# A divergence of row distributions: a casting load issued ahead of the identity matrix, six row groups on chip, and new column ranges

## Chip, cores and metric

One core of a Trainium2 chip. The metric is the device time of one execution in microseconds. The kernel before took 98.53 us (median of four executions, 97.99 to 99.74).

## What is computed

For two arrays p and q of 1024 rows and 4096 columns (fp32, each row adds up to one), the Jensen-Shannon divergence of each row:

```
m = 0.5 * (p + q)
kl_pm = np.sum(p * np.log(p / (m + 1e-8) + 1e-8), axis=-1)
kl_qm = np.sum(q * np.log(q / (m + 1e-8) + 1e-8), axis=-1)
return (0.5 * (kl_pm + kl_qm)).astype(np.float32)
```

## The kernel before

The 1024 rows are eight row groups of 128 rows, one row on each partition. Within a group the columns are cut into ranges, and four tables (L20 to L59) give the widths for each group: LOADS (what one DMA brings), LOGS (what one logarithm of p and q takes), PRODUCTS (the buffer that holds the two logarithms) and SUMS (what one sum p + q takes). The ranges of a table are numbered through all groups. For row groups 0 to 5 a range goes this way:

- **Loads.** The first HW = 2 ranges (512 and 256 columns) are loaded as fp32, p on SP's queue (L171) and q on ScalarE's (L172). All others are loaded by GpSimd with a cast to fp16 (L184 for p, L185 for q), in the order of LOADS. Each row group has a buffer of its own, so nothing but the number of loads in flight holds these back: a load waits until the eighth load before it has landed.
- **F**: TensorE adds p and q into PSUM with two matmuls against the identity (L261), in blocks of 512 columns, p and then q of each block. For the first two ranges VectorE adds instead (**a**, L236).
- **p, q**: ScalarE takes the logarithms of p and q (L277); in the first SPLIT = 5 ranges p and q are two instructions, later one over both. **c**: ScalarE takes the logarithm of the sum, from PSUM (L295).
- **u, x**: VectorE subtracts c from both logarithms (L307) and multiplies by p and q (L317). **X**: TensorE adds up the products into an accumulator of 256 columns (L356), with half the identity as weights. **f**: VectorE adds up the 256 columns (L378).

Row groups 6 and 7 (APART) avoid the subtraction. **m** multiplies the logarithms by p and q at once (L324), **s** multiplies the sum by its logarithm (L335), and **M** and **S** add both up on TensorE. The last four s and the last m are instead added up along the row by VectorE itself (L339, L328), each starting from the value of the one before. At the very end ScalarE adds up the 256 columns of row group 7 (**A**, L367), and **f7** (L372) adds VectorE's part; then SP writes the result (L466). **W** are matmuls without use (L249).

Three lists written out by hand, ACT_ORDER, PE_ORDER and DVE_ORDER (L73 to L88), fix the order on each engine; `q12 c14` means the logarithm of range 12 of LOGS and then that of range 14 of SUMS. The loop at L435 walks through the three lists and issues each entry as soon as all it depends on has been issued (`after`, L401); each engine then works strictly in its order. Logarithms share AB_BUFS = 5 buffers, logarithms of sums C_BUFS = 4. GpSimd makes the identity (L177) ahead of its first load. For row group 7 the tables are:

```
LOADS     [2048, 2048],
LOGS      [768, 1024, 896, 512, 512, 384],
PRODUCTS  [768, 1024, 896, 512, 512, 384],
SUMS      [1536, 1408, 1152],
```

Of the kernel before, what the change touches and what calls it, by code (L numbers as in the profile page):

```python
# [12 lines left out]
SW = (1536, 1536)  # L13
AW = 256
AB_BUFS = 5
C_BUFS = 4

LOADS = [  # L20
    [512, 256, 832, 960, 768, 768],
    [512, 896, 832, 768, 1088],
    [1280, 1408, 1408],
    [1152, 1408, 1536],
    [1280, 1536, 1280],
    [1408, 1408, 1280],
    [256, 1536, 1536, 768],
    [2048, 2048],
]
LOGS = [  # L30
    [512, 256, 832, 960, 768, 768],
    [512, 896, 832, 768, 1088],
    [1280, 1408, 1408],
    [1152, 1408, 1536],
    [1280, 1536, 1280],
    [1408, 1408, 1280],
    [256, 1536, 1536, 768],
    [768, 1024, 896, 512, 512, 384],
]
PRODUCTS = [  # L40
    [512, 256, 832, 1728, 768],
    [512, 896, 832, 1856],
    [1280, 1408, 1408],
    [1152, 1408, 1536],
    [1280, 1536, 1280],
    [1408, 1408, 1280],
    [1792, 1536, 768],
    [768, 1024, 896, 512, 512, 384],
]
SUMS = [  # L50
    [512, 256, 448, 384, 384, 384, 960, 768],
    [512, 896, 832, 768, 1088],
    [1280, 1408, 1408],
    [1152, 1408, 1536],
    [1280, 1536, 1280],
    [1408, 1408, 1280],
    [256, 1536, 1280, 1024],
    [1536, 1408, 1152],
]  # L59
HW = 2  # L60
SPLIT = 5

APART = 6
FUSED_M = 1
FUSED_S = 4

# [2 lines left out]


ACT_ORDER = """  # L73
p0 q0 c0 p1 q1 c1 p2 q2 c2 c3 p3 q3 c4 c5 p4 q4 c6 q5 c7 q6 c8 q7 c9 q8 c10 q9 c11 q10 c12
q11 c13 q12 c14 q13 c15 q14 c16 q15 c17 q16 c18 c19 q17 q18 c20 c21 q19 c22 q20 c23 q21
c24 c25 q22 c26 q23 q24 c27 q25 c28 q26 c29 q27 q28 c30 q29 c31 q30 q31 q32 A7
"""
PE_ORDER = """
W30 F2 F3 X0 X1 F4 F5 X2 X3 F6 X4 X5 F7 F8 X6 F9 X7 F10 X8 F11 X9 F12 X10 X11 F13 W8 X12
F14 F15 X13 F16 X14 F17 X15 F18 X16 F19 X17 F20 X18 F21 X19 F22 X20 F23 X21 F24 F25 X22  # L80
F26 S25 X23 F27 F28 S26 X24 M21 F29 S27 M22 M23 F30 F31 M24 M25 W10 M26 W4 M27 M28
"""
DVE_ORDER = """
a0 a1 u0 x0 u1 x1 u2 u3 x2 x3 u4 u5 x4 x5 u6 x6 u7 x7 u8 x8 f0 u9 x9 u10 x10 u11 x11 u12
x12 u13 f1 x13 u14 x14 u15 x15 u16 x16 f2 u17 x17 u18 x18 u19 x19 f3 u20 x20 u21 x21 u22
f4 x22 u23 s25 x23 u24 s26 x24 m21 s27 f5 m22 s28 m23 s29 m24 f6 m25 s30 m26 s31 m27 m28
m29 f7
"""  # L88


# [1 line left out]
def kernel(  # L92
# [18 lines left out]
    fp32 = mybir.dt.float32  # L111
    fp16 = mybir.dt.float16
# [18 lines left out]
    split = loads[HW][1]  # L131
# [6 lines left out]
        return r[0] >= APART  # L138

    small = ctx.enter_context(tc.tile_pool(name="small", bufs=1))  # L140
    lnp = ctx.enter_context(tc.tile_pool(name="lnp", bufs=AB_BUFS))
    mid = ctx.enter_context(tc.tile_pool(name="mid", bufs=C_BUFS))
    psp = [
# [11 lines left out]
    data = []  # L155
    for g in range(n_rg):
        t16 = small.tile([P, 2, n_cols - (split if g == 0 else 0)], fp16, tag=f"pq{g}")
        data.append(t16)

    def pq(g, c0, w):  # L160
        if g == 0:
            for i in range(HW):
                if loads[i] == (g, c0, w):
                    return early[i]
            c0 -= split
            assert c0 >= 0
        return data[g][:, :, c0 : c0 + w]

    for i in range(HW):
# [41 lines left out]
    for g in range(n_rg):  # L211
        own = [o for o in dve_order if o == ("f", g) or (fused(*o) and range_of(*o)[0] == g)]
        if g < n_rg - 1 or act_folds:
            own = [o for o in own if o[0] != "f"] + [("f", g)]
        chain[g] = own

    ab, c, s, product, acc = {}, {}, {}, {}, {}
# [102 lines left out]
    def op_m(k):  # L320
        g, c0, w = prods[k]
        u = pq(g, c0, w)
        if not fused("m", k):
            nc.vector.tensor_tensor(out=ab[k], in0=u, in1=ab[k], op=Alu.mult)  # L324
            product["M", k] = ab[k]
            return
        before, now = next_run(("m", k), g)
        nc.vector.tensor_tensor_reduce(  # L328
            out=ab[k], in0=u, in1=ab[k], scale=0.5, scalar=before,
            op0=Alu.mult, op1=Alu.add, accum_out=now,  # L330
        )

    def op_s(j):
        if not fused("s", j):
            nc.vector.tensor_tensor(out=c[j], in0=s[j], in1=c[j], op=Alu.mult)  # L335
            product["S", j] = c[j].unsqueeze(1)
            return
        before, now = next_run(("s", j), parts[j][0])
        nc.vector.tensor_tensor_reduce(  # L339
            out=c[j], in0=s[j], in1=c[j], scale=-0.5, scalar=before,  # L340
            op0=Alu.mult, op1=Alu.add, accum_out=now,
        )

    def add_up(kind, i):
# [9 lines left out]
        for n, (t, b) in enumerate(todo):  # L354
# [6 lines left out]
                stop=(kind, i) == adds[g][-1] and n == len(todo) - 1,  # L361
            )

    def op_A(g):
        folded = small.tile([P, 1], fp32, tag="folded")
        unused = small.tile([P, AW], fp16, tag="unused")
        nc.scalar.activation(out=unused, in_=acc[g][:, :AW], func=Act.Copy, accum_out=folded)  # L367
        state["folded"] = folded

    def op_f(g):  # L370
        if act_folds and g == n_rg - 1:
            nc.vector.tensor_tensor(  # L372
                out=res[:, g : g + 1], in0=state["folded"], in1=state["last"][g], op=Alu.add
            )
            return
# [25 lines left out]
    def after(kind, i):  # L401
        if kind == "F" and i - 2 >= HW:
            return [("s" if apart(parts[i - 2]) else "c", i - 2)]
        if kind == "q" and i < SPLIT:
            return [("p", i)]
        if kind in "pq" and product_of(i) >= AB_BUFS:
            return ab_free(product_of(i) - AB_BUFS)
        if kind == "c":
            return [("a" if i < HW else "F", i)] + ([c_free(i - C_BUFS)] if i >= C_BUFS else [])
        if kind == "x":  # L410
            return [("u", i)]
        if kind == "u":
            return [("c", i)] + [("q", k) for k in range(NL) if overlap(logs[k], parts[i])]
        if kind == "m":
            return [("q", k) for k in range(NL) if overlap(logs[k], prods[i])]
        if kind == "s":
            return [("c", i)]
        if kind in "XMS":
            g = range_of(kind, i)[0]
            return [(kind.lower(), i)] + ([("f", g - 2)] if g >= 2 else [])  # L420
        if kind == "W":
            return []
        if kind == "f":
            if act_folds and i == n_rg - 1:
                return chain[i][:-1] + [("A", i)]
            return chain[i][: chain[i].index(("f", i))] + adds[i]
        if kind == "A":
            return adds[i]
        return []

    accumulator(0)
    ops = dict(a=op_a, F=op_F, p=op_p, q=op_q, c=op_c, u=op_u, x=op_x, m=op_m, s=op_s, f=op_f, A=op_A)
    queues = [list(pe_order), list(act_order), list(dve_order)]
    emitted = set()
    while any(queues):  # L435
        moved = False
# [21 lines left out]
    want |= {(k.upper(), i) for k, i in want if k in "xms" and not fused(k, i)}  # L458
    want |= {("f", g) for g in range(n_rg)} | {("p", i) for i in range(SPLIT)}
    if act_folds:  # L460
        want.add(("A", n_rg - 1))
    assert emitted == want
# [34 lines left out]
```

## Time and profile before

| | |
|---|---|
| median of four executions | 98.53 us (97.99 to 99.74) |
| the profiled execution | 99.74 us, of which its span is 97.0 |
| ScalarE (ACT) busy | 90.0 us, 93% |
| VectorE (DVE) busy | 81.8 us, 84% |
| TensorE (PE) busy | 71.4 us, 74% |
| cast loads (q0) | 16.39 MB, 89.3% of the 16 DMA engines' span |
| fp32 loads (q1 and q10) | 0.79 MB, 2.7% |
| read from HBM | 33.55 MB, 346 GB/s over the span |

The profile is of one execution, with times in microseconds from the start of the span. An engine is busy while an instruction of it runs; a row of the timeline has start, length, engine, line, operation, what is written and read, and in brackets the idle time before it and what ended it. POOL is GpSimd, SP the engine that issues p's first loads and the result. A DMA's time to landing runs from its issue to its completion.

### The profile page before, as it was taken

What the parts mean: (1) busy time and instruction counts of PE and PEld (TensorE: products, weight loads), DVE (VectorE), ACT (ScalarE), POOL (GpSimd) and SP (SyncE); (2) the same over time, 40 slices, a digit from 0 to 9 for tenths busy, and PEclk for the clock granted to TensorE, in tenths of its full rate; (3) what the DMA queues carried; (4) which work ended last, traced back from release to release, by engine and by line L of the source; (5) the groups of instructions that cost most, each with busy time, mean ns of one, the idle gap of its engine ahead of it and who ended that gap; (6) DMA issues with size and microseconds to landing.
All of it is one profiled execution on the core that took longest, in us unless ns stands there. A gap on an engine that the chain in (4) does not pass through costs nothing.

```text
span 97.0 us, 1327 instructions
## 1 busy us (share of the span) xinstructions
PE 71.4 (74%) x476; PEld 46.1 (48%) x476; DVE 81.8 (84%) x87; ACT 90.0 (93%) x74; POOL 29.3 (30%) x60
## 2 busy tenths in 40 slices
PE   4996686796686948786795884884966979797750
PEld 3774343454345425553461651652643766566520
DVE  2286887999958879898979989979999999999990
ACT  3696999999999999999999999999999999999960
POOL 6943466455232234224242322325400000000000
PEclk9999999999999999999999999999999999999997
DMA  2999999999999999999999999999999999200000
GB/s 47 317 163 204 206 204 209 206 211 210 214 209 215 209 210 215 211 211 211 214 210 212 211 214 208 209 208 212 210 209 217 211 216 216 51 0 3 0 0 2
DMA packets 8502, 17.25 MB, mean 178 GB/s; under 512 B 1072, under 2 KB 3888, under 8 KB 8496
## 3 DMA queue, kind: packets, MB, share of 16 engines
q0 software_dynamic: 7776, 16.39, 89.3%
q1 hardware_dynamic: 432, 0.40, 1.5%
q10 hardware_dynamic: 288, 0.39, 1.2%
q8 instruction: 3, 0.05, 0.2%
q14 instruction: 3, 0.02, 0.1%
HBM read 33.55 MB, written 0.00 MB: 346 GB/s over the span
## 4 chain that ended last, share of the span: by engine, by line
ACT 39%; issue 22%; DVE 13%; PE 2%; ACTq 0%; DVEq 0%
ACT ab_t L277 23%; ACT c_t L295 16%; DVE ab_t L307 5%; DVE t L317 4%; DVE c_t L335 2%; DVE c_t L339 1%; PE acc_t L356 1%; PE st L261 1%; DVE ab_t L324 1%; ACT unused L367 0%; DVE res L378 0%; ACTq L295 0%; DVE res L372 0%; ACTq L492 0%; DVEq L317 0%
## 5 line engine op out<-in xcount | busy, mean ns | idle before, releaser
L277 ACT ACTIVATE ab_t<-t 128x2816 f16<-128x2816 f16 (+15 forms) x38 | 62.5, 1684 | 2.1 <-DMA t<-in_q_dram 1.0
L261 PE MATMUL st<-t,ident 128*128 128x512 f16 (+4 forms) x144 | 33.4, 350 | 9.4 <-DMA t<-in_q_dram 8.4
L307 DVE TENSOR_TENSOR ab_t<-ab_t,c_t 128x2816 f16<-128x2816 f16 (+12 forms) x25 | 29.3, 1180 | 7.7 <-ACT c_t L295 6.9
L356 PEld LDWEIGHTS <-half 128*128 128x128 f16 x268 | 25.3, 97 | 20.5 <-issue 16.7
L295 ACT ACTIVATE c_t<-st 128x1408 f16<-128x1408 f32 (+13 forms) x30 | 32.2, 1096 | 0.0
L356 PE MATMUL acc_t<-t,half 128*128 128x256 f16 (+2 forms) x200 | 23.9, 264 | 8.9 <-DVE t L317 8.6
L317 DVE TENSOR_TENSOR t<-t,ab_t 128x2816 f16<-128x2816 f16 (+11 forms) x23 | 28.2, 1234 | 1.2
L261 PEld LDWEIGHTS <-ident 128*128 128x128 f16 x144 | 13.4, 97 | 23.1 <-issue 12.8
L185 POOL DMA_DIRECT2D t<-in_q_dram x27 | 14.4, 534 | 20.7 <-DMA t<-in_q_dram 20.6
L184 POOL DMA_DIRECT2D t<-in_p_dram x27 | 14.5, 538 | 19.6 <-DMA t<-in_p_dram 19.4
L356 PE MATMUL acc_t<-ab_t,half 128*128 128x256 f16 x68 | 8.8, 270 | 2.9 <-DVE ab_t L324 2.9
L324 DVE TENSOR_TENSOR ab_t<-t,ab_t 128x1536 f16<-128x1536 f16 (+5 forms) x8 | 9.3, 1172 | 0.1
L249 PE MATMUL acc_t<-ones,ident 128*128 128x256 f16 x30 | 6.2, 403 | 1.4 <-POOL ident masks.py:199 1.4
L249 PEld LDWEIGHTS <-ident 128*128 128x128 f16 x30 | 4.3, 145 | 3.0 <-POOL ident masks.py:199 1.4
L335 DVE TENSOR_TENSOR c_t<-st,c_t 128x256 f16<-128x256 f32 (+2 forms) x3 | 3.6, 1217 | 0.0
L236 DVE TENSOR_TENSOR s<-t 128x512 f32<-128x512 f32 (+1 forms) x2 | 1.1, 558 | 2.7 <-DMA t<-in_q_dram 2.7
L339 DVE CUSTOM_DVE_ANT_0 c_t<-st,c_t,run 128x1408 f16<-128x1408 f32 (+1 forms) x2 | 3.1, 1549 | 0.0
L339 DVE CUSTOM_DVE_ANT_0 c_t<-st,c_t 128x1024 f16<-128x1024 f32 (+1 forms) x2 | 3.0, 1484 | 0.0
L249 PE MATMUL acc_t<-ones,zero 128*128 128x256 f16 x22 | 2.9, 272 | 0.0
L175 ACT ACT_TABLE_LOAD x1 | 1.3, 1283 | 1.7 <-PEq L481 1.7
L378 DVE TENSOR_REDUCE res<-acc_t 128x1 f32<-128x256 f32 x6 | 2.5, 416 | 0.0
L249 PEld LDWEIGHTS <-zero 128*128 128x128 f16 x22 | 2.1, 98 | 0.2
(24 smaller groups left out, 10.5 us busy)
## 6 DMA issues: line engine op xcount, KB each, us to landing
t<-in_p_dram POOLq DMA_DIRECT2D x5, 352.0 KB, 12.6
t<-in_q_dram POOLq DMA_DIRECT2D x5, 352.0 KB, 12.8
t<-in_p_dram POOLq DMA_DIRECT2D x4, 384.0 KB, 11.8
t<-in_q_dram POOLq DMA_DIRECT2D x4, 384.0 KB, 12.0
t<-in_p_dram POOLq DMA_DIRECT2D x4, 320.0 KB, 13.0
t<-in_q_dram POOLq DMA_DIRECT2D x4, 320.0 KB, 12.8
t<-in_p_dram POOLq DMA_DIRECT2D x2, 512.0 KB, 13.2
t<-in_q_dram POOLq DMA_DIRECT2D x2, 512.0 KB, 14.4
```

The costliest lines, as they stand in the source:

```text
L184: nc.gpsimd.dma_start(out=v[:, 0, :], in_=pv[g, :, c0 : c0 + w])
L185: nc.gpsimd.dma_start(out=v[:, 1, :], in_=qv[g, :, c0 : c0 + w])
L249: nc.tensor.matmul(out=acc[g][:, :AW], lhsT=weights, rhs=ones, start=alone, stop=alone)
L261: nc.tensor.matmul(out=st[:, b : b + m], lhsT=ident, rhs=v[:, t, b : b + m], start=t == 0, stop=t == 1,)
L277: nc.scalar.activation(out=ab[k][:, which, o : o + w], in_=pq(g, c0, w)[:, which, :], func=Act.Ln, bias=TINY, scale=SHIFT,)
L295: nc.scalar.activation(out=c_t[:, :w], in_=s[j], func=Act.Ln, bias=SHIFT * 1e-8, scale=SHIFT * 0.5)
L307: nc.vector.tensor_tensor(out=v, in0=v, in1=c[j].unsqueeze(1).to_broadcast([P, 2, parts[j][2]]), op=Alu.subtract,)
L317: nc.vector.tensor_tensor(out=into, in0=u, in1=v, op=Alu.mult)
L324: nc.vector.tensor_tensor(out=ab[k], in0=u, in1=ab[k], op=Alu.mult)
L335: nc.vector.tensor_tensor(out=c[j], in0=s[j], in1=c[j], op=Alu.mult)
L339: nc.vector.tensor_tensor_reduce(out=c[j], in0=s[j], in1=c[j], scale=-0.5, scalar=before, op0=Alu.mult, op1=Alu.add, accum_out=now,)
L356: nc.tensor.matmul(out=acc[g][:, :m], lhsT=less if kind == "S" else half, rhs=v[:, t, b : b + m], start=(kind, i) == adds[g][0] and n == 0 ...
```

## The change

Three things at the start. GpSimd issues the first casting pair (now 864 columns) ahead of the memset and select that make the identity. The fp32 loads are 576 and 384 columns wide. The useless matmuls at the start are 22 for 30.

Row groups no longer have a buffer each: six buffers (DATA_BUFS) take turns, so the loads of groups 6 and 7 wait until the last sums of groups 0 and 1 are done. Load entries **L** stand in a list of their own in the issue loop. C_BUFS is 5 for 4. All four tables are new, and the three orders follow them; products are up to 2816 columns wide, so that one buffer takes two logarithms. The logarithms split in p and q are seven ranges for five, and five s for four are added up by VectorE itself.

At the end ScalarE's A takes VectorE's part as its bias (divided by 256, since it is added in each column) and writes the result itself; f7 goes. VectorE's f6 is its last instruction.

```diff
-C_BUFS = 4
+C_BUFS = 5
+DATA_BUFS = 6
 LOADS = [
-    [512, 256, 832, 960, 768, 768],
-    [512, 896, 832, 768, 1088],
-    [1280, 1408, 1408],
+    [576, 384, 864, 1088, 1184],
+    [1280, 1536, 1280],
     [1152, 1408, 1536],
-    [1280, 1536, 1280],
-    [1408, 1408, 1280],
-    [256, 1536, 1536, 768],
+    [1024, 1024, 1024, 1024],
+    [1024, 1024, 1024, 1024],
+    [2048, 640, 128, 768, 512],
+    [1280, 1280, 1536],
     [2048, 2048],
 ]
 LOGS = [
...
-    [256, 1536, 1536, 768],
-    [768, 1024, 896, 512, 512, 384],
+    [1280, 1280, 1536],
+    [1152, 1024, 768, 512, 256, 256, 128],
 ]
 SUMS = [
...
-    [256, 1536, 1280, 1024],
-    [1536, 1408, 1152],
+    [1280, 1280, 1536],
+    [1536, 1408, 640, 512],
 ]
-SPLIT = 5
+SPLIT = 7
-FUSED_S = 4
+FUSED_S = 5
 ACT_ORDER = """
...
-c24 c25 q22 c26 q23 q24 c27 q25 c28 q26 c29 q27 q28 c30 q29 c31 q30 q31 q32 A7
+q19 c25 q20 c26 q21 c27 q22 c28 q23 c29 q24 q25 q26 q27 A7
 PE_ORDER = """
-W30 F2 F3 X0 X1 F4 F5 X2 X3 F6 X4 X5 F7 F8 X6 F9 X7 F10 X8 F11 X9 F12 X10 X11 F13 W8 X12
...
-F26 S25 X23 F27 F28 S26 X24 M21 F29 S27 M22 M23 F30 F31 M24 M25 W10 M26 W4 M27 M28
+W22 F2 X0 X1 F3 F4 X2 F5 X3 X4 F6 X5 F7 X6 F8 F9 X7 F10 X8 X9 F11 F12 X10 F13 W8 F14 X11
...
+X22 M16 F26 M17 S24 W6 F27 M18 F28 M19 F29 W4 M20 W4 M21 W3 M22 M23 M24
 DVE_ORDER = """
...
-f4 x22 u23 s25 x23 u24 s26 x24 m21 s27 f5 m22 s28 m23 s29 m24 f6 m25 s30 m26 s31 m27 m28
-m29 f7
+u22 s23 x22 m16 s24 m17 s25 f5 m18 s26 m19 s27 m20 s28 m21 s29 m22 m23 m24 m25 f6
...
+    def op_L(i):
+        g, c0, w = loads[i]
+        if g not in data:
+            t16 = datap.tile([P, 2, n_cols], fp16, tag="pq")
+            data[g] = t16
+        v = pq(g, c0, w)
+        nc.gpsimd.dma_start(out=v[:, 0, :], in_=pv[g, :, c0 : c0 + w])
+        nc.gpsimd.dma_start(out=v[:, 1, :], in_=qv[g, :, c0 : c0 + w])
+
+    op_L(HW)
     ident = small.tile([P, P], fp16, tag="ident")
     make_identity(nc, ident)
...
-    for g, c0, w in loads[HW:]:
-        v = pq(g, c0, w)
-        nc.gpsimd.dma_start(out=v[:, 0, :], in_=pv[g, :, c0 : c0 + w])
-        nc.gpsimd.dma_start(out=v[:, 1, :], in_=qv[g, :, c0 : c0 + w])
...
     def op_A(g):
-        folded = small.tile([P, 1], fp32, tag="folded")
         unused = small.tile([P, AW], fp16, tag="unused")
-        nc.scalar.activation(out=unused, in_=acc[g][:, :AW], func=Act.Copy, accum_out=folded)
-        state["folded"] = folded
+        before, now = next_run(("A", g), g)
+        nc.scalar.activation(
+            out=unused, in_=acc[g][:, :AW], func=Act.Identity, bias=before, accum_out=now
+        )
...
+        if kind == "L":
+            g = loads[i][0] - DATA_BUFS
+            return adds[g] if g >= 0 else []
```

More of the change, by code (lines that the diff above doesn't have):

```diff
@@ L30 @@
 LOGS = [
-    [512, 256, 832, 960, 768, 768],
-    [512, 896, 832, 768, 1088],
-    [1280, 1408, 1408],
+    [576, 384, 864, 1088, 1184],
+    [1280, 1536, 1280],
     [1152, 1408, 1536],
-    [1280, 1536, 1280],
+    [2048, 2048],
+    [2048, 2048],
     [1408, 1408, 1280],
-    [256, 1536, 1536, 768],
-    [768, 1024, 896, 512, 512, 384],
+    [1280, 1280, 1536],
+    [1152, 1024, 768, 512, 256, 256, 128],
 ]
 PRODUCTS = [
-    [512, 256, 832, 1728, 768],
-    [512, 896, 832, 1856],
-    [1280, 1408, 1408],
+    [576, 384, 864, 1088, 1184],
@@ L44 @@
+    [2816, 1280],
     [1152, 1408, 1536],
[L45 to L48, printed above, removed]
+    [2048, 2048],
+    [2048, 2048],
+    [2816, 1280],
+    [1280, 1280, 1536],
+    [1152, 1024, 768, 512, 256, 256, 128],
 ]
 SUMS = [
-    [512, 256, 448, 384, 384, 384, 960, 768],
-    [512, 896, 832, 768, 1088],
-    [1280, 1408, 1408],
+    [576, 384, 864, 768, 320, 1184],
+    [1280, 1536, 1280],
     [1152, 1408, 1536],
-    [1280, 1536, 1280],
+    [1024, 1024, 1024, 1024],
@@ L56 @@
+    [1024, 1024, 1024, 1024],
     [1408, 1408, 1280],
-    [256, 1536, 1280, 1024],
-    [1536, 1408, 1152],
+    [1280, 1280, 1536],
+    [1536, 1408, 640, 512],
 ]
 HW = 2
-SPLIT = 5
+SPLIT = 7
 APART = 6
 FUSED_M = 1
-FUSED_S = 4
+FUSED_S = 5
 ACT_ORDER = """
-p0 q0 c0 p1 q1 c1 p2 q2 c2 c3 p3 q3 c4 c5 p4 q4 c6 q5 c7 q6 c8 q7 c9 q8 c10 q9 c11 q10 c12
-q11 c13 q12 c14 q13 c15 q14 c16 q15 c17 q16 c18 c19 q17 q18 c20 c21 q19 c22 q20 c23 q21
-c24 c25 q22 c26 q23 q24 c27 q25 c28 q26 c29 q27 q28 c30 q29 c31 q30 q31 q32 A7
+p0 q0 c0 p1 q1 c1 p2 q2 c2 p3 q3 c3 c4 p4 q4 c5 p5 q5 c6 p6 q6 c7 q7 c8 q8 c9 q9 c10 q10
@@ L77 @@
+c11 c12 q11 c13 c14 q12 c15 c16 q13 c17 c18 q14 c19 q15 c20 c21 q16 c22 q17 c23 q18 c24
+q19 c25 q20 c26 q21 c27 q22 c28 q23 c29 q24 q25 q26 q27 A7
 """
 PE_ORDER = """
-W30 F2 F3 X0 X1 F4 F5 X2 X3 F6 X4 X5 F7 F8 X6 F9 X7 F10 X8 F11 X9 F12 X10 X11 F13 W8 X12
-F14 F15 X13 F16 X14 F17 X15 F18 X16 F19 X17 F20 X18 F21 X19 F22 X20 F23 X21 F24 F25 X22
-F26 S25 X23 F27 F28 S26 X24 M21 F29 S27 M22 M23 F30 F31 M24 M25 W10 M26 W4 M27 M28
+W22 F2 X0 X1 F3 F4 X2 F5 X3 X4 F6 X5 F7 X6 F8 F9 X7 F10 X8 X9 F11 F12 X10 F13 W8 F14 X11
@@ L82 @@
+F15 X12 F16 X13 F17 X14 F18 X15 F19 X16 X17 F20 F21 X18 X19 F22 X20 F23 X21 F24 S23 F25
+X22 M16 F26 M17 S24 W6 F27 M18 F28 M19 F29 W4 M20 W4 M21 W3 M22 M23 M24
 """
 DVE_ORDER = """
-a0 a1 u0 x0 u1 x1 u2 u3 x2 x3 u4 u5 x4 x5 u6 x6 u7 x7 u8 x8 f0 u9 x9 u10 x10 u11 x11 u12
-x12 u13 f1 x13 u14 x14 u15 x15 u16 x16 f2 u17 x17 u18 x18 u19 x19 f3 u20 x20 u21 x21 u22
-f4 x22 u23 s25 x23 u24 s26 x24 m21 s27 f5 m22 s28 m23 s29 m24 f6 m25 s30 m26 s31 m27 m28
-m29 f7
+a0 a1 u0 x0 u1 x1 u2 x2 u3 u4 x3 x4 u5 x5 u6 f0 x6 u7 x7 u8 x8 u9 x9 f1 u10 x10 u11 x11
@@ L88 @@
+u12 u13 x12 x13 f2 u14 u15 x14 x15 u16 u17 x16 x17 f3 u18 u19 x18 x19 u20 f4 x20 u21 x21
+u22 s23 x22 m16 s24 m17 s25 f5 m18 s26 m19 s27 m20 s28 m21 s29 m22 m23 m24 m25 f6
 """
@@ L140 @@
     small = ctx.enter_context(tc.tile_pool(name="small", bufs=1))
+    datap = ctx.enter_context(tc.tile_pool(name="datap", bufs=DATA_BUFS))
     lnp = ctx.enter_context(tc.tile_pool(name="lnp", bufs=AB_BUFS))
@@ L154 @@
         early.append(t32)
[L155 to L158, printed above, removed]
+    data = {}
     def pq(g, c0, w):
@@ L164, in pq @@
                     return early[i]
-            c0 -= split
-            assert c0 >= 0
+            assert c0 >= split
         return data[g][:, :, c0 : c0 + w]
@@ L213 @@
         if g < n_rg - 1 or act_folds:
-            own = [o for o in own if o[0] != "f"] + [("f", g)]
+            last = ("A" if act_folds and g == n_rg - 1 else "f", g)
+            own = [o for o in own if o[0] != "f"] + [last]
         chain[g] = own
@@ L328, in op_m @@
         nc.vector.tensor_tensor_reduce(
-            out=ab[k], in0=u, in1=ab[k], scale=0.5, scalar=before,
+            out=ab[k], in0=u, in1=ab[k], scale=0.5 * share(g), scalar=before,
             op0=Alu.mult, op1=Alu.add, accum_out=now,
@@ L337, in op_s @@
             return
-        before, now = next_run(("s", j), parts[j][0])
+        g = parts[j][0]
+        before, now = next_run(("s", j), g)
         nc.vector.tensor_tensor_reduce(
-            out=c[j], in0=s[j], in1=c[j], scale=-0.5, scalar=before,
+            out=c[j], in0=s[j], in1=c[j], scale=-0.5 * share(g), scalar=before,
             op0=Alu.mult, op1=Alu.add, accum_out=now,
@@ L362, in add_up, with share @@
             )
+    def share(g):
+        return 1.0 / AW if act_folds and g == n_rg - 1 else 1.0
     def op_A(g):
-        folded = small.tile([P, 1], fp32, tag="folded")
         unused = small.tile([P, AW], fp16, tag="unused")
-        nc.scalar.activation(out=unused, in_=acc[g][:, :AW], func=Act.Copy, accum_out=folded)
-        state["folded"] = folded
+        before, now = next_run(("A", g), g)
+        nc.scalar.activation(
+            out=unused, in_=acc[g][:, :AW], func=Act.Identity, bias=before, accum_out=now
+        )
     def op_f(g):
[L371 to L375, printed above, removed]
         before, now = next_run(("f", g), g)
@@ L423, in after @@
         if kind == "f":
-            if act_folds and i == n_rg - 1:
-                return chain[i][:-1] + [("A", i)]
             return chain[i][: chain[i].index(("f", i))] + adds[i]
         if kind == "A":
-            return adds[i]
+            return chain[i][:-1] + adds[i]
+        if kind == "L":
+            g = loads[i][0] - DATA_BUFS
+            return adds[g] if g >= 0 else []
         return []
     accumulator(0)
-    ops = dict(a=op_a, F=op_F, p=op_p, q=op_q, c=op_c, u=op_u, x=op_x, m=op_m, s=op_s, f=op_f, A=op_A)
-    queues = [list(pe_order), list(act_order), list(dve_order)]
+    ops = dict(a=op_a, F=op_F, p=op_p, q=op_q, c=op_c, u=op_u, x=op_x, m=op_m, s=op_s, f=op_f, A=op_A, L=op_L)
+    load_order = [("L", i) for i in range(HW + 1, len(loads))]
+    queues = [load_order, list(pe_order), list(act_order), list(dve_order)]
     emitted = set()
@@ L460 @@
     if act_folds:
-        want.add(("A", n_rg - 1))
-    assert emitted == want
+        want = want - {("f", n_rg - 1)} | {("A", n_rg - 1)}
+    assert {o for o in emitted if o[0] != "L"} == want and not load_order
     pe_order = [o for o in pe_order if o[0] != "W"]
```

## The prediction

> **What bounds the kernel now.** I read the page's parts 1 and 2 first, then the busy time by stage, then ScalarE's timeline beside the landing times of the loads, then the tail on ScalarE, VectorE and the TensorE.
>
> ```profile
> PE 71.4 (74%) x476; PEld 46.1 (48%) x476; DVE 81.8 (84%) x87; ACT 90.0 (93%) x74; POOL 29.3 (30%) x60
> DMA  2999999999999999999999999999999999200000
> ```
>
> ```profile
> 5.00:25.00 20.00, 14.88 (x93) 9.04 (x92) 16.93 (x25) 19.05 (x26) 9.78 (x19) 1.00 1.13 202
> 32.00:60.00 28.00, 20.95 (x136) 12.47 (x134) 25.20 (x19) 28.00 (x16) 8.97 (x17) 1.00 1.09 211
> ```
>
> The second fence is the busy time by stage: stretch, length, busy us of PE, PEld, DVE, ACT and POOL, granted clock, DMA share, GB/s. Two resources are full at once: ACT over the whole span (28.00 of 28.00 us from 32 to 60), and the DMA engines until slice 34 (82 us), at a share of 1.09 to 1.13.
>
> ```profile
> 25.45 2.02 ACT L277 ACTIVATE ab_t<-t 128x2176 f16<-128x2176 f16 x1 [0.17 <-DMA t<-in_q_dram]
> 27.38 1.06 ACT L295 ACTIVATE c_t<-st 128x1088 f16<-128x1088 f32 x1
> 28.48 2.34 ACT L277 ACTIVATE ab_t<-t 128x2560 f16<-128x2560 f16 x1
> 30.73 1.22 ACT L295 ACTIVATE c_t<-st 128x1280 f16<-128x1280 f32 x1
> 31.90 2.55 ACT L277 ACTIVATE ab_t<-t 128x2816 f16<-128x2816 f16 x1
> ```
>
> ```profile
> t<-in_q_dram POOLq DMA_DIRECT2D x1, 352.0 KB, 11.3
> ```
>
> A landing is a load's issue on POOL plus its time to landing. This is the answer on DMA issues for the q load issued at 20.50, its last figure the us to landing: 31.80. ACT starts on it at 31.90. The q loads before it landed at 25.33 and 28.38; ACT started at 25.45 and 28.48. So up to 31.9 ACT takes each range 0.10 to 0.12 us after its q half lands; it is the DMA stream that sets the pace. After that ACT falls behind the stream (q landed 35.24, start 35.58; 38.05, 39.24; later 3 us and more) and never waits again.
>
> ```profile
> 84.77 2.02 ACT L277 ACTIVATE ab_t<-t 128x2048 f16<-128x2048 f16 x1
> 86.57 1.46 ACT L295 ACTIVATE c_t<-st 128x1408 f16<-128x1408 f32 x1
> ...
> 90.39 2.87 ACT L277 ACTIVATE ab_t<-t 128x1024 f16<-128x1024 f16 x3
> 93.99 0.38 ACT L367 ACTIVATE unused<-acc_t 128x256 f16<-128x256 f32 x1 [0.73 <-PE acc_t L356]
> ```
>
> ```profile
> t<-in_q_dram POOLq DMA_DIRECT2D x1, 512.0 KB, 15.2
> ```
>
> The last q load is issued at 69.68 and takes 15.2 us: it lands at 84.88. At that moment ACT is busy with a range of the first 2048 columns until 86.57; that is the cover of the last load, 1.7 us of it. The last logarithm ends at 90.39 + 2.87 = 93.26, the output DMA is issued at 94.68.
>
> **ACT's prices.** From one start to the next, a 2816-wide logarithm from SBUF takes 2.44 us (35.58 to 38.02) and a 1408-wide one from PSUM 1.22 (38.02 to 39.24). With 0.8333 ns per element that is 0.095 and 0.055 us on top. Laid in ACT_ORDER with the landings, these two prices give every ACT start of the kernel before to about 0.15 us (31.90, 61.85 for 61.80, 93.12 for 93.26 at the end), so I use them for the kernel after.
>
> **What the skill says.** "ScalarE: Activation LUTs", What ACT_TABLE_LOAD costs: 0.833 ns per element, and about 93 ns for a [128,1] pointer operand. The first agrees with the rows above; the second is my price for the new bias of the last fold, which no row shows. "Trainium Kernel Development and Optimization", Key Constraints: DMAs from SP, ACT and POOL run on the same 16 engines and interleave. The trace agrees: from 4.0 to 4.5 us ACT's queue holds 57% of the engines and POOL's 46%. "DMA: Bandwidth & Descriptors", Rules for kernel authors: a cast needs GpSimd, so fp32 loads are the only ones SP and ACT can bring early.
>
> **The change, part by part.**
>
> *Pair of loads ahead of the identity.* POOL's first load starts at 1.43; the memset starts at 0.74, so the pair is issued 0.7 us earlier, and the identity comes after two DMA issues (0.67 + 0.54), near 2.5 instead of 1.3. Behind it wait the first matmuls and half and less on VectorE. VectorE's next work is at 4.35 (wait for a load), TensorE's first real matmul at 7.39: hidden; uncovered it would cost 1.2. Warm-up: 8 matmuls fewer at 0.206 us (30 in 6.19), 1.65; 2.5 + 22 x 0.206 ends at 7.0, before the first sum can start. Nothing.
> But the engines are already full when this pair could profit: 2.0 to 4.6 us show shares of 84 to 108%, and packets of POOL's queue start at 4.1 and follow without a gap. An earlier issue shares the engines, it doesn't add any. What it could save is slowness: the first 1664-byte packets take 155 to 188 ns where the same size takes 144 later, over 16 packets per engine some 0.35 us. Bounds 0 and 0.4; I take 0.2.
>
> *More fp32 columns.* 576 + 384 for 512 + 256: 192 columns of p and q. Early 2048-byte packets take 84 ns and 1024-byte ones 46, so 38 ns per KB; each engine gets 16 packets larger by 256 bytes and 16 by 512: 16 x 9.5 + 16 x 19 = +0.46 us. Off POOL's queue go 384 x 1.15 ns = -0.44 us (pace below). The DMA total stays.
>
> *Pace of the stream.* From the landing at 8.50 of the first casting pair to 84.88 there are 52 loads with 62,336 columns: 76.38 us, that is 0.09 us per load and 1.15 ns per column (2048 wide takes 2.42 to 2.44, 512 wide 0.56 to 0.70). After: 52 loads with 61,888 columns, 75.85 us. The pair itself lands at 8.50 + 0.46 + 0.07 (864 for 832 wide) - 0.2 = 8.83. Last landing: 84.68 (84.5 to 84.9).
>
> *ACT up to the last load.* q2 starts 0.1 after its landing, 8.93. From there to the logarithm of the second sum of row group 7 (c27, 1408 wide) there are 86,112 elements x 0.8333 = 71.76, 24 logarithms from SBUF x 0.095, 25 from PSUM x 0.055: 75.42, with 0.3 of small waits on loads early on. ACT is there at 84.65. Five logarithms fewer in the whole kernel are worth 0.4 us, contained in this.
>
> *The new wait.* Both c27 (columns 1536 to 2944) and the next logarithm (1152 to 2176) cross column 2048, so both need the last load. Only one range of 1152 columns stands before them, where the old kernel had 768 and 1024. c27 comes from TensorE: after the landing three matmuls (0.19 each, from 12 in 2.33) and two handovers of about 0.1: 0.8. It starts at 84.68 + 0.8 = 85.5, a wait of 0.8 us on ACT; behind it stand all of ACT's last work, and s27 on VectorE. So what ACT gained is handed to this wait.
>
> *After it.* c27 1.23, then 1.80, 0.59, 1.38, 0.48, 0.95, 0.52, 0.52, 0.31: 7.78, so the last logarithm ends at 93.26, the same as before. VectorE has from c27's end s27 1.60, then 1.14, 0.82, 0.88, 0.68, 0.61, 0.34, 0.34, 0.42 (2048-element rows of 1.22 less 0.08 overlap, and so on): 6.83 and a gap, done 0.65 after ACT's last logarithm. The fold A7 now waits for that product's accumulator: start 0.13 later, then 0.38 + 0.09 + 0.19, and 0.06 to the output DMA: 1.50 behind the last logarithm, where the old kernel needs 1.42. f6 in the same time on VectorE (0.56) is hidden by it.
>
> *Six row groups, C_BUFS 5, larger products.* The first load of group 6 waits for group 0's last sums, which TensorE ends near 20 us; it is issued near 60. Nothing; 40 us would have to go first. More c buffers: no ACT wait on a buffer is in the waits, so nothing. VectorE: four u/x less, one m more, 0.16 fixed each: -0.5, early fp32 ranges +0.4.
>
> **Sum.** 93.26 + 1.50 = 94.76 against 94.68: +0.1 us on a span of 97.0. That execution took 99.74 (span and 2.7 around it), the most of the four; I put the difference on the median, 98.53: 98.6.
>
> **Rivals.**
> 1. *The stream comes sooner, the last wait goes away.* For it: that execution took more than the other three, so loads may be quicker in those; one early load took 1.85 us where its twin took 1.31. Against: the shares are at 110% from 5 to 32 us. Without the wait the end is 8.83 + 0.1 + 83.2 (ACT from q2 on) + 0.3 + 1.5 = 93.9: -0.8, 97.8; with the pair at 8.5 it is 97.4. It needs the stream 0.8 us faster, and the old kernel would win a third of it.
> 2. *Slower: POOL's queue runs dry at the small loads of row group 5* (640, 128, 768, 512). Loads wait for the eighth before them, and the first packets come 2.7 us after an issue (1.43 to 4.1). When group 6's first load is issued, the seven between hold 0.83 + 2 x 0.24 + 2 x 0.97 + 2 x 0.68 = 4.6 us, and engines spread by up to 2 us around a landing: the cover is just used up. Every bubble goes through c27 to the end: 0.3 is 98.9, 1.0 is 99.6. From a last landing of 84.6 on the change is a loss, from 85.6 by 1%.
> 3. *The buffers of six groups hold loads back.* 40 us of slack speak against it; a load of 2.4 us late would give 101.
>
> **Chances.** 0.55 for the forecast (98.2 to 99.0), 0.25 for rival 1, 0.18 for rival 2, 0.02 for rival 3. The range 97.4 to 99.5 leaves out the far ends of 1 and 2. One per cent, 1 us, is about what a measurement of this kernel can tell from no change. Faster by more takes most of rival 1: 0.21. Slower by more takes the larger bubbles of rival 2 and a little of the forecast: 0.19. Within: 0.60.
>
> **What would show it.** POOL's first load near 0.75, its q half landing near 8.8; ACT waits for q2 as before, then has no wait above 0.2 until c27, whose idle time is 0.5 to 1.0, released by TensorE's sum (L266) and behind it the last load; last landing 84.5 to 84.9. No wait at c27 would mean rival 1, a landing gap after the 512-wide loads rival 2. The prediction is wrong if the stream's total changes, or if ACT's start moves by more than the stream's.

## The result, and the profile after

The kernel after takes 97.85 us (median of 43 executions, 97.59 to 99.46), the kernel before 98.52 (64 executions): ratio 0.9938, 95% interval [0.9923, 0.9953]. It is 0.6 us faster, less than one per cent, but clearly so; I had forecast 98.6, no change. The time around the span is 1.8 us in most executions of both kernels, and in the experiments the kernel before has a median span of 96.6; the execution that the prediction was read from (97.0 and 2.7) was slower than most. One of the experiments' profiles, e13's, is of a disturbed execution (span 99.2); only its first ten microseconds are used.

The page of the kernel after, parts 1 and 2:

```profile
PE 68.7 (71%) x461; PEld 44.6 (46%) x461; DVE 81.0 (84%) x84; ACT 89.6 (93%) x69; POOL 29.3 (31%) x60
DMA  2999999999999999999999999999999999300000
GB/s 45 359 214 211 211 210 215 208 212 211 211 213 213 206 210 211 207 211 210 207 213 212 216 207 198 203 211 213 213 215 213 213 215 215 70 0 0 0 0 2
```

```profile
5.00:25.00 20.00, 14.53 (x96) 9.09 (x94) 16.57 (x18) 20.00 (x22) 7.49 (x15) 1.00 1.10 211
32.00:60.00 28.00, 21.11 (x138) 13.00 (x136) 24.07 (x22) 28.00 (x17) 10.56 (x20) 1.00 1.12 209
```

Busy times have hardly moved. From 5 to 25 us (the second fence is the busy time by stage) ScalarE is busy all of the 20.00 us, where it was 19.05, and the engines bring 211 GB/s for 202. What is new is the third slice of the GB/s row (4.8 to 7.2 us): 214, where the kernel before has 163:

```profile
GB/s 47 317 163 204 206 204 209 206 211 210 214 209 215 209 210 215 211 211 211 214 210 212 211 214 208 209 208 212 210 209 217 211 216 216 51 0 3 0 0 2
```

The casting loads run at full rate from their first packets.

GpSimd's start and the landing of the first casting q half (DMA issues: the last figure is us from issue to landing), first in the kernel before, then in the kernel after:

```profile
1.43 0.67 POOL L184 DMA_DIRECT2D t<-in_p_dram  x1
2.10 0.54 POOL L185 DMA_DIRECT2D t<-in_q_dram  x1
```

```profile
t<-in_q_dram POOLq DMA_DIRECT2D x1, 208.0 KB, 6.4
```

```profile
1.24 0.66 POOL L180 DMA_DIRECT2D t<-in_p_dram  x1 [0.79 <-POOLq L489]
1.89 0.54 POOL L181 DMA_DIRECT2D t<-in_q_dram  x1
```

```profile
t<-in_q_dram POOLq DMA_DIRECT2D x1, 216.0 KB, 5.6
```

The first load starts at 1.24, only 0.19 us sooner than before (1.43), not 0.7. But its q half lands at 1.89 + 5.6 = 7.49, 1.0 us sooner than before (8.50), though 0.2 MB more fp32 goes ahead of it. (A landing is known to 0.05 us in this way.)

ScalarE's start and end:

```profile
4.26 1.26 ACT L282 ACTIVATE ab_t<-t 128x576 f16<-128x576 f32 x2 [1.11 <-DMA t<-in_p_dram]
...
7.24 1.72 ACT L282 ACTIVATE ab_t<-t 128x864 f16<-128x864 f16 x2
8.87 0.87 ACT L300 ACTIVATE c_t<-st 128x864 f16<-128x864 f32 x1
...
82.24 2.12 ACT L282 ACTIVATE ab_t<-t 128x2304 f16<-128x2304 f16 x1
84.64 1.34 ACT L300 ACTIVATE c_t<-st 128x1408 f16<-128x1408 f32 x1 [0.29 <-PE st L266]
...
90.12 2.40 ACT L282 ACTIVATE ab_t<-t 128x1024 f16<-128x1024 f16 x4
93.18 0.47 ACT L377 ACTIVATE unused<-acc_t,run 128x256 f16<-128x256 f32 x1 [0.66 <-PE acc_t L362]
```

The row at 7.24 is the first casting pair, p and q in one stretch with no wait between, where the kernel before waited 0.80 us for q:

```profile
8.51 0.90 ACT L277 ACTIVATE ab_t<-t 128x832 f16<-128x832 f16 x1 [0.80 <-DMA t<-in_q_dram]
```

The row at 84.64 is c27, and it waits for TensorE as forecast, but 0.29 us. On the way there it waits twice more, 0.21 us each (at 30.07 and 80.89), where I had forecast no wait above 0.2. The last load's q half:

```profile
t<-in_q_dram POOLq DMA_DIRECT2D x1, 512.0 KB, 16.4
```

Issued at 67.43, it lands at 83.83, and c27 starts 0.81 behind it. The last logarithm ends at 92.52 (before: 93.26), the output is issued at 93.77 (94.68).

### The profile page after: what moved, and what is told of

Its sections match the earlier page's. It is cut to its first block, busy times and chain, and to the rows that moved or that the text cites. A ratio compares the mean times of both kernels' runs of the same rounds, so it can differ in the third digit from the quotient of the medians.

```text
span 96.1 us, 1290 instructions
## 1 busy us (share of the span) xinstructions
PE 68.7 (71%) x461; PEld 44.6 (46%) x461; DVE 81.0 (84%) x84; ACT 89.6 (93%) x69; POOL 29.3 (31%) x60
## 4 chain that ended last, share of the span: by engine, by line
DMA 65%; issue 12%; ACT 8%; DVE 8%; PE 3%; POOL 1%; DVEq 0%; ACTq 0%; POOLq 0%
DMA t<-in_q_dram 59%; ACT ab_t L282 6%; DMA t<-in_p_dram 6%; DVE ab_t L312 2%; DVE t L322 2%; PE st L266 2%; DVE c_t L345 2%; DVE ab_t L329 1%; ACT c_t L300 1%; PE acc_t L362 1%; POOL t L180 1%; ACT unused L377 0%; DVEq L500 0%; ACTq L500 0%; DVEq L322 0%
## 5 line engine op out<-in xcount | busy, mean ns | idle before, releaser
L282 ACT ACTIVATE ab_t<-t 128x2560 f16<-128x2560 f16 (+15 forms) x35 | 61.1, 1777 | 1.3 <-DMA t<-in_p_dram 1.1
L266 PE MATMUL st<-t,ident 128*128 128x512 f16 (+6 forms) x138 | 32.6, 357 | 6.2 <-DMA t<-in_q_dram 5.2
L362 PEld LDWEIGHTS <-half 128*128 128x128 f16 x266 | 25.2, 97 | 23.3 <-issue 17.4
L312 DVE TENSOR_TENSOR ab_t<-ab_t,c_t 128x2048 f16<-128x2048 f16 (+10 forms) x23 | 28.8, 1269 | 7.0 <-ACT c_t L300 4.3
L362 PE MATMUL acc_t<-t,half 128*128 128x256 f16 (+1 forms) x192 | 23.4, 268 | 13.2 <-DVE t L322 13.0
L300 ACT ACTIVATE c_t<-st 128x1024 f16<-128x1024 f32 (+10 forms) x28 | 31.0, 1132 | 0.5 <-PE st L266 0.5
L322 DVE TENSOR_TENSOR t<-t,ab_t 128x2048 f16<-128x2048 f16 (+8 forms) x21 | 27.4, 1325 | 0.6
L362 PE MATMUL acc_t<-ab_t,half 128*128 128x256 f16 (+2 forms) x74 | 9.2, 267 | 1.5 <-DVE ab_t L322 0.8
L329 DVE TENSOR_TENSOR ab_t<-t,ab_t 128x2560 f16<-128x2560 f16 (+6 forms) x9 | 9.6, 1088 | 0.5 <-ACT ab_t L282 0.4
L345 DVE CUSTOM_DVE_ANT_0 c_t<-st,c_t,run 128x1408 f16<-128x1408 f32 (+2 forms) x3 | 3.3, 1103 | 0.3 <-ACT c_t L300 0.3
L345 DVE CUSTOM_DVE_ANT_0 c_t<-st,c_t 128x1536 f16<-128x1536 f32 x2 | 3.5, 1751 | 0.0
```

Of the source, the lines that this page charges most:

```text
L266: nc.tensor.matmul(out=st[:, b : b + m], lhsT=ident, rhs=v[:, t, b : b + m], start=t == 0, stop=t == 1,)
L282: nc.scalar.activation(out=ab[k][:, which, o : o + w], in_=pq(g, c0, w)[:, which, :], func=Act.Ln, bias=TINY, scale=SHIFT,)
L300: nc.scalar.activation(out=c_t[:, :w], in_=s[j], func=Act.Ln, bias=SHIFT * 1e-8, scale=SHIFT * 0.5)
L312: nc.vector.tensor_tensor(out=v, in0=v, in1=c[j].unsqueeze(1).to_broadcast([P, 2, parts[j][2]]), op=Alu.subtract,)
L322: nc.vector.tensor_tensor(out=into, in0=u, in1=v, op=Alu.mult)
L345: nc.vector.tensor_tensor_reduce(out=c[j], in0=s[j], in1=c[j], scale=-0.5 * share(g), scalar=before, op0=Alu.mult, op1=Alu.add, accum_out=now,
```

## Experiments

Two theories at first. A: issuing the pair ahead of the identity is what brings the casting stream forward. B: the first profile of the kernel before caught an execution with a slow start, and the gain lies elsewhere. Ratios are to the kernel before.

**e1, the kernel before again.** No edit.

> The kernel before once more, for its profile. Theory A (the pair issued ahead of the identity brings the whole casting stream forward): the first casting q half lands near 8.5 us and the last load near 84.9 again, as in the first profile of this kernel. Theory B (the first profile of the kernel before caught an execution whose casting stream started slowly): the first q half lands near 7.5 to 7.8 and the last load near 83.9 to 84.2, as in the kernel after, and its first packets take about 144 ns each.

The q half lands at 8.49, the last load at 85.09; span 96.5, time 98.25. The slow start is a property of that kernel: B falls.

**e2, the pair alone.**

```diff
+    load(*loads[HW])
     ident = small.tile([P, P], fp16, tag="ident")
     make_identity(nc, ident)
...
-    for g, c0, w in loads[HW:]:
+    for r in loads[HW + 1 :]:
-W30 F2 F3
+W22 F2 F3
```

> The kernel before with the first pair of casting loads ahead of the identity and 22 warm-up matmuls, nothing else. Theory A: most of the gain of the whole change, ratio 0.990 to 0.996, first casting q half landing 0.5 to 1.0 us sooner. Theory B: the POOL queue starts its first DMA only 0.2 us sooner (1.24 for 1.43), so ratio 0.998 to 1.002.

0.9965 [0.9946, 0.9985], q half landing at 7.80: about half of the gain, and between the two ranges expected.

**e3, the kernel after with the pair behind the identity.**

```diff
-    op_L(HW)
     ident = small.tile([P, P], fp16, tag="ident")
     make_identity(nc, ident)
+    op_L(HW)
-W22 F2
+W30 F2
```

> The kernel after with its first pair behind the identity again and 30 warm-up matmuls. Theory A: the gain is gone, ratio to the kernel before 0.998 to 1.004. Theory B: the gain stays, ratio 0.992 to 0.996.

1.0016 [0.9991, 1.0040]: the gain is gone. The profiled execution, at 98.13 us, is faster than most of e3's 22 (median 98.47). Its POOL rows and the landing of the q half:

```profile
1.02 0.29 POOL masks.py:199 TENSOR_SCALAR_AFFINE_SELECT ident<-ident 128x128 f16<-128x128 f16 x1
1.42 0.67 POOL L180 DMA_DIRECT2D t<-in_p_dram  x1
2.09 0.54 POOL L181 DMA_DIRECT2D t<-in_q_dram  x1
```

```profile
t<-in_q_dram POOLq DMA_DIRECT2D x1, 216.0 KB, 6.6
```

8.69, against 7.49 with the pair ahead. What the engines moved from 4.9 to 7.2 us, first in the kernel after, then in e3 (packets, MB, share of 16 engines):

```profile
q0 software_dynamic: 297, 0.47, 112.4%
```

```profile
q0 software_dynamic: 270, 0.43, 106.8%
```

In both, the casting packets begin when the fp32 loads drain (4.4 to 4.6 us); the issue does not move their beginning. Behind the identity the engines do 9% less in the next 2.3 us, though this alone is no mark of a late issue: e6 and e12 below, with an early one, have 271 and 273 packets there. The packet records show where it is felt: in the kernel after all 256 packets of the pair have ended at 7.23; in e3 at 7.5 all but eight have, and the last six of these end one after another, 0.12 to 0.14 us apart, up to 8.41, as on one engine that is a load behind the rest. The landings say the same. A trace has sixteen marks of each landing, as many as there are engines, and the load has landed with the last of them. For the first q half, in us:

| mark | kernel after | e5 | e14 | e3 |
|---|---|---|---|---|
| 8th of 16 | 7.35 | 7.27 | 7.29 | 7.28 |
| 15th | 7.49 | 7.65 | 8.24 | 7.97 |
| 16th | 7.50 | 8.21 | 8.26 | 8.69 |

The middle of the marks is no later in e3; only the last ones are. And e3's last mark stays 0.6 to 0.8 us behind the one before it in every load up to 24.2 us, where in the kernel after the last two are never more than 0.03 apart in these loads after the first. I read a mark as one engine's, which the traces do not name.

**e4, more cover for the last load.**

```diff
-    [1152, 1024, 768, 512, 256, 256, 128],
+    [1152, 896, 896, 512, 256, 256, 128],
...
-q19 c25 q20 c26 q21 c27 q22 c28 q23 c29 q24 q25 q26 q27 A7
+q19 c25 q20 c26 q21 q22 c27 c28 q23 c29 q24 q25 q26 q27 A7
...
-m18 s26 m19 s27 m20 s28
+m18 s26 m19 m20 s27 s28
```

> The kernel after with logarithms of row group 7 cut at column 2048 (1152, 896, 896 for 1152, 1024, 768) and both ranges of the first load ahead of the sum's logarithm that needs the last load. If the wait on the last load (0.29 us in the profile of the kernel after) is what holds the end: that wait is gone, ScalarE's last logarithm ends 0.2 to 0.3 us sooner, ratio to the kernel before 0.990 to 0.992. If VectorE, which has no idle time to speak of at the end, holds it: no gain, ratio 0.993 to 0.997, because its sums come later.

0.9954 [0.9931, 0.9976], no gain. c27's wait is gone, but a wait comes back behind it:

```profile
85.75 2.04 ACT L300 ACTIVATE c_t<-st 128x1408 f16<-128x1408 f32 x2
87.56 1.82 ACT L282 ACTIVATE ab_t<-t 128x1792 f16<-128x1792 f16 x1
89.60 0.60 ACT L300 ACTIVATE c_t<-st 128x512 f16<-128x512 f32 x1 [0.23 <-PE st L266]
...
93.41 0.47 ACT L377 ACTIVATE unused<-acc_t,run 128x256 f16<-128x256 f32 x1 [0.92 <-PE acc_t L362]
```

0.23 at c29 and 0.92 for 0.66 before the fold give back the 0.29. VectorE, busy 8.60 of the 9.20 us from 84.6 on (8.51 in the kernel after), has as much to do in that stretch as ScalarE; that it is what holds the end was not tried by itself.

**e5 and e6, work on POOL ahead of the pair.** e5 puts the identity's memset ahead of the pair and leaves the select behind it; e6 puts a memset of 128 x 512 ahead.

```diff
+    nc.gpsimd.memset(idle, 0.0)
     op_L(HW)
```

> The kernel after with the identity's memset ahead of the first pair and its select behind it. If the select just ahead of the first load is what makes one DMA engine start its casting packets 1.2 us late: the first q half lands near 7.5 to 7.8 as in the kernel after, ratio to the kernel before 0.992 to 0.996. If it is any work on POOL ahead of the first load: it lands near 8.5 to 8.7, ratio 0.998 to 1.003.

> The kernel after with a memset of 128 x 512 on POOL ahead of the first pair, the identity still behind the pair, so that the first load is issued near 1.5 us or later. If the time of the issue decides: the first q half lands at 8.5 or later, ratio 0.998 to 1.004. If the neighbourhood of the select decides: 7.5 to 7.8, ratio 0.992 to 0.996.

e5 0.9932 [0.9903, 0.9961], landing 8.22; e6 0.9937 [0.9909, 0.9965], landing 7.93. Neither tells what it was meant to: the memsets ran beside the start-up of the first DMA, which was issued at 1.26 and 1.27. The times stay with the early pair. e5's one landing is as late as e14's below, and that execution, 97.99 us, is not slower for it.

**e7, the old fp32 loads in the kernel after.**

```diff
-    [576, 384, 864, 1088, 1184],
+    [512, 256, 864, 1280, 1184],
```

> The kernel after with fp32 loads of 512 and 256 columns and ranges of 864, 1280, 1184 behind them. If the fp32 columns cost the DMA engines as much as they save POOL's queue (0.46 against 0.44 us): last landing within 0.2 us of the kernel after, ratio to the kernel before 0.992 to 0.997. If the larger fp32 loads are a part of the gain (no casting packet over 280 ns at the start of the kernel after, more than ten in the kernel before): slow packets come back, ratio 0.997 to 1.001.

1.0000 [0.9983, 1.0018]: the gain is gone again, and slow packets are back (15 of the first pair's took over 280 ns; in the kernel after none did). The pair landed at 7.70 all the same, and the last load at 84.01, 0.2 from the kernel after: the DMA total is indeed the same. ScalarE came to both q halves too soon:

```profile
7.68 0.92 ACT L282 ACTIVATE ab_t<-t 128x864 f16<-128x864 f16 x1 [0.31 <-DMA t<-in_q_dram]
...
10.79 1.27 ACT L282 ACTIVATE ab_t<-t 128x1280 f16<-128x1280 f16 x1 [0.25 <-DMA t<-in_q_dram]
```

Its profiled span (96.2) is shorter than its median (96.7), so this profile shows the kind of wait and not all of its size. Nor does every early wait cost time: in e8, next, ScalarE waits 0.37 us at 9.25, and the gain is kept.

**e8, seven row groups on chip.** DATA_BUFS = 7.

> The kernel after with buffers for seven row groups for six. Nothing waits for a buffer, so no change from the kernel after: ratio to the kernel before 0.992 to 0.996, first load of row group 6 issued at the same place in the stream. If the wait of POOL ahead of row group 6 (0.5 us in the profile of the kernel after) costs anything: ratio below 0.992.

0.9922 [0.9896, 0.9949], as the kernel after within the intervals. The number of buffers costs nothing that can be seen.

**e9 and e10, fp32 columns and the start as a whole, on the kernel before.** e9 widens the fp32 loads only; e10 has e2's edit as well. Everything else is the kernel before's.

```diff
-    [512, 256, 832, 960, 768, 768],
+    [576, 384, 832, 768, 768, 768],
```

> The kernel before with fp32 loads of 576 and 384 columns (behind them 832, 768, 768, 768), nothing else of the change. Theory C (the pair and the wider fp32 loads work together: ScalarE has enough early columns to reach the first casting pair after it has landed, and only then does an earlier pair count): alone it gives little, ratio 0.998 to 1.002. Theory D (the two effects are independent): 0.994 to 0.997, as much as the kernel after wins over the one with the old fp32 loads.

> The kernel before with both edits of the start, the pair ahead of the identity and fp32 loads of 576 and 384 columns, but the old ranges of groups 1 to 7, a buffer for each group, and the old end. If the start is all of the gain: ratio 0.992 to 0.995, no wait of ScalarE for the first casting q half. If the new ranges and buffers are needed too: 0.996 to 0.999.

e9 0.9983 [0.9952, 1.0015]; e10 0.9914 [0.9885, 0.9942], 97.68 us, just below the range expected. The start alone is all of the gain. The beginning of e10:

```profile
6.71 0.51 ACT L299 ACTIVATE c_t<-s 128x384 f16<-128x384 f32 x1
7.12 1.67 ACT L281 ACTIVATE ab_t<-t 128x832 f16<-128x832 f16 x2
8.70 0.90 ACT L299 ACTIVATE c_t<-st 128x448 f16<-128x448 f32 x2
```

No wait at the q half (landed 7.60). With one row for each state of the start:

| pair, fp32 columns | old ranges, buffers and end | new ones |
|---|---|---|
| behind the identity, 512 + 256 | 1 | not run |
| ahead, 512 + 256 | 0.9965 (e2) | 1.0000 (e7) |
| behind, 576 + 384 | 0.9983 (e9) | 1.0016 (e3) |
| ahead, 576 + 384 | 0.9914 (e10) | 0.9938 (the kernel after) |

On the old ranges the two edits win 0.35 and 0.17% alone and 0.86% together; that this is more than their sum is likely and not shown, since the intervals leave about 0.5% of room on a difference of 0.34. On the new ranges neither keeps the gain without the other.

In each row with both the new ranges, buffers and end come out 0.24 to 0.35% slower than the old ones. The intervals of each pair touch or overlap, so no single row proves it; three of three point the same way.

**e11 and e12, the smaller fp32 load first.** 384 + 576 for 576 + 384, in e12 with e4's cover.

> The kernel after with the two fp32 loads exchanged, 384 columns first and 576 behind. ScalarE starts on the first load near 3.6 to 3.9 us for 4.26. If ScalarE's own start and work set the end: 0.3 us sooner, ratio to the kernel before 0.989 to 0.992. If the landing of the last load sets it (c27 is 0.8 us behind it): ScalarE waits 0.3 us more at c27 and the ratio stays 0.992 to 0.995.

> The same with the logarithms of row group 7 cut at column 2048, so that ScalarE has more work ahead of the one that needs the last load. If last landing and ScalarE's start are the two bounds: 0.3 to 0.5 us sooner than the kernel after, ratio 0.987 to 0.991. If VectorE's work after the last sum's logarithm sets the end: 0.992 to 0.996, as with more cover alone.

e11 0.9948 [0.9921, 0.9975], e12 0.9998 [0.9963, 1.0033]. ScalarE starts at 3.75, 0.5 sooner, and it is not worth anything: in e11 c27 waits (0.32), at 84.57 for 84.64. An earlier start of ScalarE is lost at the last load, as that expectation's second half had it. e12 missed both ranges expected of it. That it is slower than e4 I can't explain; its profile shows 0.48 us of waiting for the second, larger fp32 load.

**e13 and e14, the issue delayed without the identity.** As e6, with 704 and 1536 columns.

> The kernel after with a memset of 128 x 704 on POOL ahead of the first pair, so that its first load is issued near 1.46 us, as late as behind the identity, with the identity still behind the pair. If the time of the issue decides where the pair lands: first q half at 8.3 to 8.7, ratio to the kernel before 0.998 to 1.003. If the identity's select ahead of it decides: 7.5 to 7.9, ratio 0.992 to 0.996.

> The same with 128 x 1536, first load issued near 2.3 us. If the landing follows the issue one for one from the kernel after: first q half near 8.6. If an issue after about 1.4 us costs a fixed 1 us and no more (the casting packets wait for the fp32 ones, which drain at 4.5 to 4.9 us, in any case): near 8.5. If both add up: 9.3 or later, ratio above 1.005.

e13 0.9984 [0.9958, 1.0010], e14 1.0003 [0.9975, 1.0030]. Against the kernel after, the gain goes with 0.12 us of delay, and a delay of 0.8 us costs no more. e13, then e14:

```profile
1.36 0.66 POOL L180 DMA_DIRECT2D t<-in_p_dram  x1
2.02 0.54 POOL L181 DMA_DIRECT2D t<-in_q_dram  x1
2.54 0.23 POOL masks.py:197 MEMSET ident<- 128x128 f16 x1
```

```profile
2.06 0.66 POOL L180 DMA_DIRECT2D t<-in_p_dram  x1
2.71 0.54 POOL L181 DMA_DIRECT2D t<-in_q_dram  x1
```

The q halves land at 2.02 + 6.3 = 8.32 and 2.71 + 5.5 = 8.21. So it isn't the identity's select ahead of the load; it is the time of the issue, and not in proportion. First issue at 1.24 to 1.27: landing 7.49 to 8.22 in eleven profiles (ten at 8.00 or before). At 1.36 to 2.06: 8.21 to 8.69 in six. From the 8th mark of that landing to the last it is 0.1 to 0.9 us in the eleven and 0.9 to 1.6 in the six, so the groups touch. What happens between 1.27 and 1.36 that leaves engines behind was not found.

**e15, the start and the new end on the old ranges.** e10 with the kernel after's fold (bias, no f7).

> The kernel before with both edits of the start and the new end (ScalarE's fold takes VectorE's part as its bias, no f7), old ranges, eight buffers. From the profiles the new end is 1.25 us behind the last logarithm for 1.42, so 0.15 us sooner than the start alone: ratio to the kernel before 0.988 to 0.992. If VectorE's last product, which the fold now waits for, takes that back: 0.990 to 0.994, no different from the start alone.

0.9948 [0.9922, 0.9973]: no better than e10, and above both ranges expected. On the old ranges the fold waits for VectorE's last product, which is 768 elements wide there and 256 in the kernel after:

```profile
93.71 0.47 ACT L378 ACTIVATE unused<-acc_t,run 128x256 f16<-128x256 f32 x1 [1.16 <-DVE run L334]
```

e10, 97.68 us, has the lowest median, 0.2 below the kernel after; their intervals overlap, so it is at least as good, and not shown to be better.

## Why the prediction was wrong

*The step that failed* is the term for the early issue: "An earlier issue shares the engines, it doesn't add any. What it could save is slowness: ... some 0.35 us. Bounds 0 and 0.4; I take 0.2." The rule of "shares, doesn't add" was drawn from the mean share of the engines, and the term came out too small. In time the early issue alone is worth 0.43 us with the old fp32 columns (e2 against the kernel before measured beside it, 98.04 for 98.47), and with the wider ones 0.60 (e9 to e10) and 0.62 (e3 to the kernel after). In the profiles the pair was put at 8.83, 0.33 us later than before; it landed at 7.49, 1.0 us sooner, and without the early issue (e3) at 8.69: 1.2 us of landing, six times what I took. What the mean share hid is in the marks of e3: the engines were full on average, with a share of 106.8%, but the last mark came 1.4 us behind the middle one. The first profile has a trace of it that I booked as slow packets only: the q half landed 1.67 us after the p half, where the size pays for 1.05. It is no sure sign: in e1 the p half is as late as the q half, and they are 1.06 apart.

*The size of the issue's move* was wrong the other way: 0.19 us for 0.7. The first DMA has 0.79 us of idle time ahead of it (the row at 1.24), where a memset has 0.29.

*The fp32 columns* were mis-sized too, at +0.46 us on the first pair. The casting packets do begin that much later (4.11 us in the kernel before, 4.56 in the kernel after), but the pair does not land later: in the three pairs of profiles that differ by the columns (e1 and e9, e2 and e10, e7 and the kernel after) it lands 0.20, 0.20 and 0.21 us sooner with the wider ones, and the pair's packets over 280 ns fall from 18, 12 and 15 to 4, 2 and 0. The last load lands 0.86 and 0.98 us sooner on the old ranges, 0.18 on the new ones. I also gave these columns no other value, and they may have one: they are the work that ScalarE does until the first q half lands. 960 columns last to 7.24, 768 to 6.47. That is cover for an early pair, and of e2, e9 and e10 only e10, which has both, leaves no wait there. Which of the two, the landings or the cover, the columns are worth is not separated by these runs.

*The last landing* beat its forecast by 0.85 us (83.83 for 84.68), and the early issue is the smaller part of that: e3, without it, has 84.16. There the forecast without the 0.2 is 9.03 for the pair and 84.88 for the last load; e3's pair landed at 8.69, and its stream took 75.47 us from there for 75.85.

*The sum after the last load* held. c27 starts 0.81 behind the landing (forecast 0.8), the last logarithm ends 7.88 behind c27's start (7.78), the output follows 1.25 later (1.50; the fold started 0.66 behind it for 0.78, and the read of its sum runs 0.1 beside it). From the landing to the output's issue: 9.94 us, forecast 10.08. With the last landing at 84.68 instead of 83.83, this sum gives 94.62 for the output's issue, and I predicted 94.76.

*What became of the 1.2 us.* The landings of the kernel after lead those of e3 by 1.2 us (7.49 for 8.69) up to the load at 23.03 (e3: 24.22). The next p half lands at 25.41 and 25.61, and from there to the end the lead is mostly 0.2 to 0.5 (83.83 for 84.16); a load near 51 us leads by 1.0, and one at 79.58 lands 0.4 behind e3's. From 23.2 to 23.7 us the kernel after has one packet of another queue among its loads:

```profile
q0 software_dynamic: 48, 0.11, 110.9%
q8 instruction: 1, 0.02, 11.8%
```

It is an instruction fetch of 16 KB, and it holds its engine for 0.95 us. Of the load that lands at 25.41, fifteen marks have come by 24.40; the last is alone, 1 us behind. In e3 the fetch comes at the same time, and that load's last marks are 24.93, 25.55 and 25.60: one engine was late before, now a second is beside it, and the landing hardly moves (1.39 after the one before; in the kernel after 2.38). It is no price of an early pair. Of the nine profiles on the new ranges, e13's left aside, that have a fetch between 23.3 and 24.2 us, seven have 2.3 to 2.6 us between these two landings, e14 with its late pair among them (2.28), and two have 1.4 (e3, and e12 with an early pair). In e7 the fetch comes at 26.80, and it is 1.39. The fetches can't be moved by an edit of the order, so none of this was tried.

*What stays open* is how the early issue reaches the end. The profiled executions of e3 and the kernel after are 0.25 us apart (98.13 and 97.88), the medians 0.62. e14's, with the pair at 8.21, took 97.95 where its median is 98.45, and e5's, with 8.22, took 97.99. So the profiles show an engine that falls behind, and account for less than half of the time. The rest is in executions that were not profiled: the middle half of e3's lies from 98.2 to 98.9, that of the kernel after from 97.8 to 97.9.

*Rivals.* Rival 1 (the stream comes sooner) is what the profile shows: it asked for 0.8 us at the last load and got 0.85, gave 93.9 for the output's issue, and 93.77 was measured. I gave it a quarter for want of a cause. Its wait "goes away" only in part (0.29 us), and e4 shows that removing the rest gains nothing. Rival 2: group 6's first load was issued at 60.20, its p half landed 1.55 us after the load before, which is its normal time; no bubble. Rival 3: e8, nothing.

*The range* of 97.4 to 99.5 held the time; the sign did not hold.

## What to carry to other kernels

The stream of loads was here as late as its latest engine: read landings load by load at the start, and where a load takes longer than its size pays for, look there before concluding from a full DMA share that nothing can be gained. An earlier load and work that covers the consumer until it lands belong together, so test two such edits in all four combinations: here neither alone shows all of the gain. When a late landing is forecast, check the forecast landing by itself: here the sum behind it was right to 0.15 us. And before a profile is taken for a kernel, compare its time with the kernel's median.

## What was unexpected

A casting load first issued at 1.24 to 1.27 us landed at 7.5 to 8.2, at 1.36 or later at 8.2 to 8.7, with packets beginning at the same time in both (4.4 to 4.6 us with 576 + 384). Issued at 1.24 (the kernel after) or at 2.06 (e14), it had its first packet only at 4.56 and 4.43, while packets of the fp32 loads ran from 1.7 to 5.1 and 5.2. A last mark that is late stays late, load after load, for 15 us (e3). An instruction fetch (16 KB, 0.95 us on one engine) goes with a landing that is 1 us late. The last fold takes 0.09 us more (0.47 for 0.38) with a pointer bias, and with Identity for Copy; 0.09 is the figure for the bias in the Trainium skill, "ScalarE: Activation LUTs", What ACT_TABLE_LOAD costs.
